# Two changes of order and one of shape in a two-layer streaming encoder: the sums for seven products, and the mixer's kernel product in column quarters

## The chip, the cores and the metric

The kernel runs on one core of one Trainium2 chip. The metric is the device time of one launch in microseconds (us), taken as the median of three runs; one further execution was profiled.

## What is computed

One inference step of a two-layer streaming encoder, for a prompt of 1024 positions and a sample of 64, 1088 columns in all, with 1024 channels. Layer 0 mixes tokens by sliding-window attention, layer 1 by a complex-diagonal state space (S5). Each layer ends in a gated feed-forward part with a causal depthwise convolution of width 3:

```python
def conv_ffn(h, prev, w_up, conv_w, conv_b, w_down):
    up = h @ w_up
    full = jnp.concatenate([prev.astype(up.dtype), up], axis=1)
    ...
    y = (jax.nn.gelu(c[..., :D_FF]) * c[..., D_FF:]) @ w_down
```

The mixer of layer 1 has 64 groups of 16 channels, with one state of 64 complex numbers per group:

```python
    xr = jnp.einsum('blgi,gpi->blgp', u_blk, bbr)
    xi = jnp.einsum('blgi,gpi->blgp', u_blk, bbi)
    ...
    y = jnp.einsum('blgp,gip->blgi', sr, cr) - jnp.einsum('blgp,gip->blgi', si, ci)
```

The kernel computes it over chunks of eight positions, and needs tables for that: the response of every group over eight steps (16 by 128 numbers a group, here called the kernel product, `kps`), and the transposed input weights (`wps`).

## The kernel before, in words

**Products.** The engines are called PE (TensorE, the matrix engine), DVE (VectorE), ACT (ScalarE), POOL (GpSimd) and SP (SyncE, which only issues transfers here). The 1088 columns are worked in three blocks of 384, 384 and 320. A float32 product is made of three fast ones (`mm3`, L223 to L225), with weights and data split into a high and a low part (L216, L194 for the weights). PSUM has six banks for these products and two small tiles, `sm0` and `sm1`.

**The feed-forward part** (`ffn`, L340). The up-projection goes over 22 tiles f: the products of rows f and 22 + f, their evacuation into `u`, the convolution (`conv`, L419 to L421), GELU, the product of both halves (L437) and its write to DRAM as `gd` (L438, L439). In layer 1 the tiles from f = 5 are made by seven products in place of eight (`seven`; L508 to L521 are the evacuations on DVE). The down-projection over the first 768 columns is also made by seven products (`pair`); for that it needs sums of quarters of its weights (`sums_w`, L355 to L362) and of `gd` (`sums_g`, L367 to L374).

**The sums.** Each is a generator with two steps. The first issues a load (L355, L367). The second is four DVE operations in place (L358 to L361, L370 to L373) and a write to DRAM (`sd`, `td`). `aside` is called twice in each tile, once between the two convolutions and once behind the gate, and calls `sums(j)` with j counting the calls. `starts` says at which j a generator's first step is taken: odd j for the weights, even j for `gd`; `jobs` says at which j the second is. Before, that is j + 1. Loads and writes are on SP's queue in layer 0 and on POOL's in layer 1. The tile `jt` of layer 0 has one place for the weights' sums and two for those of `gd`; in layer 1 `jw` and `jg` have one place each, so a load has to wait until the write before it has landed.

**The tables of layer 1's mixer** (`ssm_prep`, L1098) are made beside layer 0's up-projection, as its `side` work: eight blocks q of four pairs of groups, each with `ssm_chunk` (L1016) and `ssm_toeplitz` (L1086). In `ssm_chunk` DVE makes `ct` (L1034 to L1039) and, with `cmul`, `w` (L882 to L887); ACT writes the input weights of each pair of groups into a block-diagonal tile `bd` (L1048). PE then multiplies: eight products of `bd[:, g, c]` with `ct[:, g, c]`, which add up into one 128 x 128 result `kps` (L1062). Each stationary operand is 128 columns wide and holds numbers in 32 of them, the other columns being zero. DVE takes the result into `kt` (L1066, L1067), which goes to DRAM. Eight transposes of `w` (L1073) follow, c = 0 into `sm0`, the bank that `kps` had, and c = 1 into `sm1`; ACT copies them (L1074) and SP writes them to `prm` (L1075).

**What sets the order.** A planner fixes the order of the instructions on every engine and queue when the program is built. Each instruction gets the number of the moment at which it was written (`cur_priority`, which counts up); among those that its reckoning holds ready, an engine takes the lowest number. `later(LOW)` adds 1500 to the numbers of the side work. `order(x, first)` keeps x behind `first` on its engine without a wait on the chip. Tiles with the same tag share their places.

Of the kernel before, what the change touches and what calls it, by code (L numbers as in the profile page):

```python
# [8 lines left out]
F32 = mybir.dt.float32  # L9
F32R = mybir.dt.float32r  # L10
I32 = mybir.dt.int32
AF = mybir.ActivationFunctionType
# [3 lines left out]
P = 128  # L16
# [6 lines left out]
KF = DFF // P  # L23
# [20 lines left out]
class Core:  # L44
# [72 lines left out]
    @contextmanager  # L117
    def later(self, n):

        p = self.tc.cur_priority  # L120
        self.tc.cur_priority = p + n
        yield
        self.tc.cur_priority = p

    @contextmanager
    def boundary(self, nsq=2):
# [84 lines left out]
    behind = ()  # L211
# [128 lines left out]
    def ffn(self, i, h, rb, after, side=None, beside=lambda: None, x=None, g=None):  # L340

        nc, tc, a = self.nc, self.tc, self.a
# [37 lines left out]
        jobs = {}  # L380

        def sums(j):

            for x in jobs.pop(j, []):
                next(x, None)
            if j in starts:
                x = starts[j]
                next(x)
                jobs[j + 1] = [x]

        def u_tile(m):
            u = self.t4([P, T + 4], "u")
# [50 lines left out]
        def aside():  # L443

            j = next(turns) + 1
            if side is not None and j <= SIDE:
                with self.later(LOW):
                    next(side, None)
            sums(j - 1)
# [84 lines left out]
        for f in range(1, KF):  # L534
# [14 lines left out]
                us = up([f, KF + f, f + 1])  # L549
            gate(f, us)  # L550
            aside()
        for j in range(2 * KF, 2 * KF + 2):
            sums(j)
        if i == 1:
            ts_ctx.__exit__(None, None, None)
# [61 lines left out]
        def part(c):  # L617

            t0, n = BLK[2]
            k0 = KCUT[c]  # L620
            out = {}
            for sz, tag in GT[c]:
                if tag == "big":
                    x = self.big([P, 2, sz, n], "gt")
                else:
                    x = self.blk.tile([P, 2, sz, n], F32R, name="gt", tag=tag, bufs=4 if tag == "blkA" else 2)
                for j in range(0, sz, 2):
                    raw = self.t4([P, 2, n], "gr")
                    nc.sync.dma_start(raw, gd[:, k0 + j:k0 + j + 2, t0:])
                    split_units(x, slice(j, j + 2), raw)  # L630
                    for z in range(2):
                        out[k0 + j + z] = x, j + z
                k0 += sz
            return out
# [24 lines left out]
        with self.boundary():  # L659
# [3 lines left out]
            gs = part(0)  # L663
# [228 lines left out]
    def ssm_small(self):  # L892

        nc, a = self.nc, self.a
# [5 lines left out]
        sm = self.prep.tile([P, 1024], F32, name="sm0", tag="sm").rearrange("p (a q) -> p a q", a=32)  # L900
# [79 lines left out]
        c, s = cs, sn  # L980
        for k in range(10):
# [8 lines left out]
            c, s = (ph[:, 0, k - 2], ph[:, 1, k - 2]) if k > 1 else (ta[:, 8], ta[:, 9])  # L990
# [3 lines left out]
        for t, n, p0 in ((self.tq[:, :, 0:32], 16, 0), (self.tp[:, :, 18:36], 9, 4)):  # L994
            t = t.rearrange("p q (c k) -> p q c k", c=2)
            V.memset(t[:, :, 0, 0:1], 1.0)
            V.memset(t[:, :, 1, 0:1], 0.0)
            w, k = 1, p0
            while w < n:
# [3 lines left out]
                m = [m[:, i, :NPR * u].rearrange("p (q j) -> p q j", j=u) for i in range(2)]  # L1003
                self.cmul(V, [t[:, :, i, w:w + u] for i in range(2)], [t[:, :, i, 0:u] for i in range(2)], y, m)
                w, k = w + u, k + 1
        self.bd_ = self.prep.tile([P, 4, 2, P], F32, name="bd", tag="sm")
        V.memset(self.bd_, 0.0)
        self.dv = self.prep.tile([P, 24], F32, name="dv")
        nc.sync.dma_start(self.dv[:, 16:], a["s_d"])
# [6 lines left out]
    def ssm_chunk(self, q):  # L1016

        nc, a = self.nc, self.a
        G, V = nc.gpsimd, nc.vector
        gs = slice(4 * q, 4 * q + 4)  # L1020
        if q == 0:
            z = self.pt([P, 8, 112], "z0")
            G.memset(z, 0.0)
            nc.sync.dma_start(self.kd[:, 0:7].rearrange("(b p) t i -> p b (t i)", p=P), z)
        two = lambda t, o, n: (t[:, gs, o:o + n], t[:, gs, o + n:o + 2 * n])
        (ac, as_), (bbr, bbi), (cr, ci) = (two(self.tq, o, 16) for o in (0, 32, 64))
        (pr, pi), (bc, bs) = two(self.tp, 0, 9), two(self.tp, 18, 9)

        ct = self.pt([P, 4, 2, 9, 16], "ct")
        m = self.pm2()  # L1030
        m1, m2 = (m[:, i].rearrange("p (g t i) -> p g t i", t=9, i=16) for i in range(2))
        wide = lambda x: x[:, :, None, :].to_broadcast([P, 4, 9, 16])
        tall = lambda x: x[:, :, :, None].to_broadcast([P, 4, 9, 16])
        V.tensor_mul(m1, wide(cr), tall(pr))  # L1034
        V.tensor_mul(m2, wide(ci), tall(pi))
        V.tensor_sub(ct[:, :, 0], m1, m2)
        V.tensor_mul(m1, wide(cr), tall(pi))
        V.tensor_mul(m2, wide(ci), tall(pr))
        V.scalar_tensor_tensor(ct[:, :, 1], m1, -1.0, m2, op0=ALU.mult, op1=ALU.subtract)  # L1039
        oc = self.pt([P, 4, 2, 16, 8], "oc")  # L1040
        for c in range(2):
            nc.scalar.activation(oc[:, :, c], ct[:, :, c, 1:9].rearrange("p g t i -> p g i t"), AF.Copy)
        nc.sync.dma_start(self.prm[:, gs, OC:OC + 256], oc.rearrange("p g c i t -> p g (c i t)"))

        for e, r in enumerate((slice(0, 64), slice(64, 128))):
            o = self.bd_[r, 0, 0, 16 * e:16 * e + 1]
            o = bass.AP(tensor=o.tensor, offset=o.offset, ap=[o.ap[0], [2 * P + 32, 4], [P, 2], [1, 16]])
            nc.scalar.activation(o, self.tq[r, gs, 32:64].rearrange("p g (c j) -> p g c j", c=2), AF.Copy)  # L1048

        w = self.pt([P, 4, 2, 16, 8], "w")  # L1050
        m = self.pm2()
        m = [m[:, i, :512].rearrange("p (g j s) -> p g j s", j=16, s=8) for i in range(2)]
        row = lambda x: x[:, :, :, None].to_broadcast([P, 4, 16, 8])
        pwr = lambda x: x[:, :, None, 0:8].to_broadcast([P, 4, 16, 8])
        self.cmul(V, (w[:, :, 0], w[:, :, 1]), (row(bbr), row(bbi)), (pwr(pr), pwr(pi)), m)
        yield

        kps = self.sm_ps("kps", 0)
        behind = self.last_mm
        for g in range(4):  # L1060
            for c in range(2):
                x = nc.tensor.matmul(kps[:, :P], self.bd_[:, g, c], ct[:, g, c, 0:8].rearrange("p t i -> p (t i)"),  # L1062
                                     start=g + c == 0, stop=g + c == 4)
                self.order(x, behind)
        kt = self.prep.tile([P, P], F32, name="kt")
        V.scalar_tensor_tensor(kt[:, 0:16], self.dv[:, :16], self.dv[:, 16 + q:17 + q], kps[:, 0:16], op0=ALU.mult, op1=ALU.add)  # L1066
        V.tensor_copy(kt[:, 16:], kps[:, 16:P])  # L1067
        nc.sync.dma_start(self.kd[q * P:q * P + P, 7:].rearrange("j t i -> j (t i)"), kt)
        b3 = self.pt([P, 4, 2, P], "b3")
        for c in range(2):  # L1070
            wps = self.sm_ps("wps", c)
            for g in range(4):
                self.order(nc.tensor.transpose(wps[:, g * P:g * P + P], w[:, g, c].rearrange("p j s -> p (j s)"), self.ident), behind)  # L1073
            nc.scalar.activation(b3[:, :, c], wps.rearrange("p (g n) -> p g n", g=4), AF.Copy)  # L1074
        nc.sync.dma_start(self.prm[:, gs, OW:OW + 256], b3.rearrange("p g c n -> p g (c n)"))  # L1075

        tab = self.pt([P, 4, 2, 144], "tab")
        m = self.pm2()
        m = [m[:, i].rearrange("p (g b a) -> p g b a", b=9, a=16) for i in range(2)]
        v = lambda i: tab[:, :, i].rearrange("p g (b a) -> p g b a", a=16)  # L1080
        self.cmul(G, (v(0), v(1)), (wide(ac), wide(as_)), (tall(bc), tall(bs)), m)
        G.tensor_copy(tab[:, :, :, 129:138], tab[:, :, :, 0:9])
        for c, o in enumerate((OCO, OSI)):
            nc.gpsimd.dma_start(self.prm[:, gs, o:o + 138], tab[:, :, c, 0:138])
# [515 lines left out]
```

## Time and profile before

| | |
|---|---|
| median of three runs | 2259.97 us (2258.63 to 2260.15) |
| the profiled execution's own time | 2264.88 us |
| its span | 2263.1 us |
| PE, DVE, ACT, POOL busy | 2201.7, 1688.5, 1019.2, 415.2 us |
| instructions | 36074 |

The span runs from the first to the last instruction on the core; the time of the execution holds 1.8 us more around it. Busy time counts each engine by itself. A product's duration runs until its results are out, so products that follow each other overlap, and their cost is the distance of their starts. The columns of a timeline are the start, the duration, the engine and line, the operation, its output and inputs, the part of the array that it uses (rows*columns), the moving operand and the count of instructions put together; [idle before <- what ended it] stands behind those that found the engine idle. One float32 product that isn't split shows as two instructions.

### The profile page before, as it was taken

What the parts mean: (1) busy time and instruction counts of PE and PEld (TensorE: products, weight loads), DVE (VectorE), ACT (ScalarE), POOL (GpSimd) and SP (SyncE); (2) the same over time, 40 slices, a digit from 0 to 9 for tenths busy, and PEclk for the clock granted to TensorE, in tenths of its full rate; (3) what the DMA queues carried; (4) which work ended last, traced back from release to release, by engine and by line L of the source; (5) the groups of instructions that cost most, each with busy time, mean ns of one, the idle gap of its engine ahead of it and who ended that gap; (6) DMA issues with size and microseconds to landing.
All of it is one profiled execution on the core that took longest, in us unless ns stands there. A gap on an engine that the chain in (4) does not pass through costs nothing. (4 is left out here: it accounts for less than half of the span.)

```text
span 2263.1 us, 36074 instructions
## 1 busy us (share of the span) xinstructions
PE 2201.7 (97%) x13875; PEld 2122.4 (94%) x13875; DVE 1688.5 (75%) x2954; ACT 1019.2 (45%) x1839; POOL 415.2 (18%) x474
## 2 busy tenths in 40 slices
PE   8999999999999999999998899999999999999997
PEld 8987789999999999999996799999999999989997
DVE  8677647989877777667767855588997787686764
ACT  5255747422333343455534641263544444355543
POOL 5322004200042423000200034352011011100000
PEclk9999999999999999999998999999999999999999
DMA  5100014656345565887749888652266577578773
GB/s 195 37 21 29 16 65 151 242 191 211 107 138 185 178 203 179 259 288 222 227 164 339 262 286 300 234 166 74 96 233 218 213 287 258 193 250 278 222 256 99
DMA packets 208124, 428.48 MB, mean 189 GB/s; under 512 B 23312, under 2 KB 114224, under 8 KB 205008
## 3 DMA queue, kind: packets, MB, share of 16 engines
q1 hardware_dynamic: 175648, 326.56, 44.0%
q0 software_dynamic: 23984, 95.12, 11.6%
q10 hardware_dynamic: 8320, 4.49, 0.9%
q8 instruction: 109, 1.79, 0.3%
q14 instruction: 63, 0.52, 0.1%
HBM read 297.75 MB, written 128.37 MB: 188 GB/s over the span
## 5 line engine op out<-in xcount | busy, mean ns | idle before, releaser
L223 PE MATMUL mm<-hl,whl 128*128 128x384 f32 (+1 forms) x1960 | 643.8, 329 | 7.7 <-DVE hl L306 3.1
L225 PE MATMUL mm<-hh,whl 128*128 128x384 f32 (+1 forms) x1960 | 641.1, 328 | 2.3 <-DVE whl L216 2.3
L224 PE MATMUL mm<-hh,whl 128*128 128x384 f32 (+1 forms) x1960 | 642.2, 328 | 0.0
L223 PEld LDWEIGHTS mm<-hl,whl 128*128 128x128 f32 x1960 | 368.4, 188 | 10.8 <-DVE hl L306 4.5
L225 PEld LDWEIGHTS mm<-hh,whl 128*128 128x128 f32 x1960 | 368.4, 188 | 2.9 <-DVE whl L216 2.9
L224 PEld LDWEIGHTS mm<-hh,whl 128*128 128x128 f32 x1960 | 368.7, 188 | 0.0
L216 ACT ACTIVATE whl<-raw 128x1024 fp32r<-128x1024 f32 x202 | 212.9, 1058 | 339.1 <-PE mm L225 176.4
L216 DVE TENSOR_TENSOR whl<-raw,whl 128x1024 fp32r<-128x1024 f32 x202 | 254.4, 1263 | 96.7 <-ACT whl L216 96.2
L223 PE MATMUL mm<-gt,whl 128*128 128x384 f32 (+1 forms) x968 | 318.5, 329 | 7.9 <-DVE y L613 3.6
L225 PE MATMUL mm<-gt,whl 128*128 128x384 f32 (+1 forms) x968 | 316.9, 328 | 0.7 <-DVE whl L216 0.7
L224 PE MATMUL mm<-gt,whl 128*128 128x384 f32 (+1 forms) x968 | 317.3, 328 | 0.0
L223 PEld LDWEIGHTS mm<-gt,whl 128*128 128x128 f32 x968 | 182.9, 189 | 10.5 <-DVE y L613 4.9
L225 PEld LDWEIGHTS mm<-gt,whl 128*128 128x128 f32 x968 | 182.7, 189 | 1.0 <-DVE whl L216 1.0
L224 PEld LDWEIGHTS mm<-gt,whl 128*128 128x128 f32 x968 | 182.8, 189 | 0.0
L194 DVE TENSOR_TENSOR whl<-raw,whl 128x1024 fp32r<-128x1024 f32 x84 | 96.3, 1153 | 73.0 <-ACT whl L193 72.4
L193 ACT ACTIVATE whl<-raw 128x1024 fp32r<-128x1024 f32 x84 | 82.6, 986 | 126.8 <-DMA raw<-sd 51.0
L419 ACT ACTIVATE t<-u,ppt 128x1090 f32<-128x1090 f32 x88 | 114.2, 1298 | 50.6 <-DVE u L521 24.6
L420 DVE SCALAR_TENSOR_TENSOR t<-u,ppt,t 128x1090 f32<-128x1090 f32 x88 | 123.6, 1406 | 9.8 <-ACT t L419 9.1
L421 DVE SCALAR_TENSOR_TENSOR t<-u,ppt,t 128x1090 f32<-128x1090 f32 x88 | 123.4, 1403 | 0.4
L563 DVE TENSOR_TENSOR gt<-gr,gt 128x768 fp32r<-128x768 f32 (+2 forms) x106 | 90.2, 880 | 10.7 <-ACT gt L562 10.1
L331 POOL TENSOR_TENSOR y<-y,xl 128x768 f32<-128x768 f32 (+1 forms) x16 | 31.3, 1954 | 354.0 <-DVE y L328 288.0
L562 ACT ACTIVATE gt<-gr 128x768 fp32r<-128x768 f32 (+2 forms) x106 | 78.3, 771 | 39.5 <-DMA gr<-gd 30.2
(390 smaller groups left out, 4181.0 us busy)
## 6 DMA issues: line engine op xcount, KB each, us to landing
raw<-in_w_up SPq DMA_DIRECT2D x88, 512.0 KB, 4.3
raw<-in_w_down SPq DMA_DIRECT2D x74, 512.0 KB, 4.5
raw<-sd SPq DMA_DIRECT2D x40, 512.0 KB, 4.6
sj<-in_w_up POOLq DMA_DIRECT2D x68, 256.0 KB, 6.4
su<-sj POOLq DMA_DIRECT2D x34, 512.0 KB, 5.8
raw<-su SPq DMA_DIRECT2D x34, 512.0 KB, 4.8
pm<-prm SPq DMA_DIRECT2D x32, 522.0 KB, 8.2
gr<-td SPq DMA_DIRECT2D x40, 384.0 KB, 5.9
```

The lines of the kernel that those rows point to most:

```text
L193: nc.scalar.activation(w[:, 0], raw, AF.Copy)
L194: nc.vector.tensor_sub(w[:, 1], raw, w[:, 0].bitcast(F32))
L216: x = nc.scalar.activation(w[:, 0], raw, AF.Copy), nc.vector.tensor_sub(w[:, 1], raw, w[:, 0].bitcast(F32))
L223: nc.tensor.matmul(out, w[:, 0, sl], xl, start=start, stop=False)
L224: nc.tensor.matmul(out, w[:, 0, sl], xh, start=False, stop=False)
L225: self.last_mm = nc.tensor.matmul(out, w[:, 1, sl], xh, start=False, stop=stop)
L331: x = by[q].tensor_add(yq, yq, xs[q])
L419: nc.scalar.activation(t, u[:, 0:T + 2], AF.Identity, bias=cb(m), scale=cw(0, m))
L420: nc.vector.scalar_tensor_tensor(t, u[:, 1:T + 3], cw(1, m), t, op0=ALU.mult, op1=ALU.add)
L421: self.last_conv = nc.vector.scalar_tensor_tensor(t, u[:, 2:T + 4], cw(2, m), t, op0=ALU.mult, op1=ALU.add)
L562: nc.scalar.activation(x[:, 0, u], raw, AF.Copy)
L563: nc.vector.tensor_sub(x[:, 1, u], raw, x[:, 0, u].bitcast(F32))
```

## The change

- `due(p)` is new: instructions written under it get the number p, and the count goes on behind it as if they had not been there.
- The second step of a sum is taken at j + 2 in place of j + 1; the last round of calls is one longer.
- `bd` shrinks from 128 to 32 columns for each g and c, and L1048 writes it with a plain slice.
- The kernel product of g goes into partitions 32 g to 32 g + 31 of `kps`, from a stationary operand of 32 columns. c is now the outer loop, each quarter adds up two products, and all eight have one number.
- The transposes of c = 1 come first, with the number of the kernel product plus 12; those of c = 0 have that number plus 50.

```diff
@@ -123,6 +123,14 @@
     @contextmanager
+    def due(self, p):
+
+        q = self.tc.cur_priority
+        self.tc.cur_priority = p
+        yield
+        self.tc.cur_priority = q
@@ -386,7 +394,7 @@
                 x = starts[j]
                 next(x)
-                jobs[j + 1] = [x]
+                jobs[j + 2] = [x]
@@ -549,7 +557,7 @@
             aside()
-        for j in range(2 * KF, 2 * KF + 2):
+        for j in range(2 * KF, 2 * KF + 3):
             sums(j)
@@ -1003,7 +1011,7 @@
-        self.bd_ = self.prep.tile([P, 4, 2, P], F32, name="bd", tag="sm")
+        self.bd_ = self.prep.tile([P, 4, 2, 32], F32, name="bd", tag="sm")
@@ -1043,9 +1051,7 @@
         for e, r in enumerate((slice(0, 64), slice(64, 128))):
-            o = self.bd_[r, 0, 0, 16 * e:16 * e + 1]
-            o = bass.AP(tensor=o.tensor, offset=o.offset, ap=[o.ap[0], [2 * P + 32, 4], [P, 2], [1, 16]])
-            nc.scalar.activation(o, self.tq[r, gs, 32:64].rearrange("p g (c j) -> p g c j", c=2), AF.Copy)
+            nc.scalar.activation(self.bd_[r, :, :, 16 * e:16 * e + 16], self.tq[r, gs, 32:64].rearrange("p g (c j) -> p g c j", c=2), AF.Copy)
@@ -1057,20 +1063,25 @@
-        for g in range(4):
-            for c in range(2):
-                x = nc.tensor.matmul(kps[:, :P], self.bd_[:, g, c], ct[:, g, c, 0:8].rearrange("p t i -> p (t i)"),
-                                     start=g + c == 0, stop=g + c == 4)
+
+        due = self.tc.cur_priority
+        for c in range(2):
+            for g in range(4):
+                with self.due(due):
+                    x = nc.tensor.matmul(kps[32 * g:32 * g + 32, :P], self.bd_[:, g, c], ct[:, g, c, 0:8].rearrange("p t i -> p (t i)"),
+                                         start=c == 0, stop=c == 1)
                 self.order(x, behind)
...
         b3 = self.pt([P, 4, 2, P], "b3")
-        for c in range(2):
+        for c in (1, 0):
             wps = self.sm_ps("wps", c)
             for g in range(4):
-                self.order(nc.tensor.transpose(wps[:, g * P:g * P + P], w[:, g, c].rearrange("p j s -> p (j s)"), self.ident), behind)
+                with self.due(due + (50 if c == 0 else 12)):
+                    x = nc.tensor.transpose(wps[:, g * P:g * P + P], w[:, g, c].rearrange("p j s -> p (j s)"), self.ident)
+                self.order(x, behind)
             nc.scalar.activation(b3[:, :, c], wps.rearrange("p (g n) -> p g n", g=4), AF.Copy)
```

## Rows read from the trace of the kernel before

**Rows 1.** The page, part 1: busy time, share of the span, instructions.

```profile
PE 2201.7 (97%) x13875; PEld 2122.4 (94%) x13875; DVE 1688.5 (75%) x2954; ACT 1019.2 (45%) x1839; POOL 415.2 (18%) x474
```

**Rows 2.** Waits of PE, 590 to 905 us: total us, times, longest.

```profile
PE wps L1073 <- DVE kt L1067: 4.4, 3, 1.7
PE wps L1073 <- DVE w L887: 2.9, 3, 1.2
```

**Rows 3.** Waits of DVE, 1790 to 2040 us.

```profile
DVE jg L370 <- DMA jg<-gd: 31.3, 7, 7.2
```

**Rows 4.** Waits of PE, 1310 to 2010 us.

```profile
PE mm L223 <- DVE u L520: 4.9, 3, 2.1
```

**Rows 5.** Timeline of PE, 656 to 664 us: start, us, what, [idle before].

```profile
656.09 0.39 PE L1062 MATMUL kps<-ct,bd 128*128 128x128 f32 x2
...
656.46 0.38 PE L1062 MATMUL kps<-ct,bd 128*128 128x128 f32 x2
...
657.57 0.31 PE L223 MATMUL mm<-hl,whl 128*128 128x320 f32 x1
...
658.59 0.31 PE L224 MATMUL mm<-hh,whl 128*128 128x320 f32 x1
...
662.66 0.63 PE L1073 MATMUL wps<-ident,w 128*128 128x128 f32 x4 [1.68 <-DVE kt L1067]
```

**Rows 6.** Timeline of PE, 1280 to 1309 us: half-column runs (128*64).

```profile
1283.22 1.16 PE L1249 MATMUL p<-U,pm 128*64 128x137 f32 x16
1284.31 0.73 PE L1309 MATMUL p<-U,pm 128*128 128x137 f32 x4
1284.88 0.56 PE L230 MATMUL p<-ppt,ident 128*128 128x238 f32 x2
...
1288.73 0.69 PE L1249 MATMUL p<-U,pm 128*64 128x137 f32 x8
1289.35 0.74 PE L1309 MATMUL p<-U,pm 128*128 128x137 f32 x4
```

**Rows 7.** Timeline of PE, 120.3 to 121.4 us.

```profile
120.53 0.31 PE L225 MATMUL gq<-hh,whl 128*128 128x320 f32 x1
120.78 0.65 PE L796 MATMUL po<-ptT,vt 128*64 128x256 f32 x4
```

**Rows 8.** Timeline of PE, 776 to 783 us.

```profile
776.35 0.31 PE L225 MATMUL mm<-hh,whl 128*128 128x320 f32 x1
777.88 0.33 PE L1073 MATMUL wps<-ident,w 128*128 128x128 f32 x1 [1.22 <-DVE w L887]
...
781.65 0.63 PE L1073 MATMUL wps<-ident,w 128*128 128x128 f32 x4 [1.44 <-DVE kt L1067]
```

**Rows 9.** Timeline of PE, 772.2 to 772.9 us.

```profile
772.36 0.38 PE L1062 MATMUL kps<-ct,bd 128*128 128x128 f32 x2
```

**Rows 10.** Timeline of DVE, 764 to 784 us.

```profile
771.86 0.69 DVE L884 TENSOR_TENSOR w<-m 128x512 f32<-128x512 f32 x1 [2.81 <-DMA prm<-oc]
...
777.13 0.69 DVE L887 TENSOR_TENSOR w<-m 128x512 f32<-128x512 f32 x1
...
781.25 0.26 DVE L1067 COPY kt<-kps 128x112 f32<-128x112 f32 x1
```

**Rows 11.** Tile jt: ns min/median/max, first and last start in us.

```profile
L358 DVE TENSOR_TENSOR jt<-jt x11: 679/691/694, 404.8 to 566.5; 128x512 f32<-128x512 f32 x11
```

**Rows 12.** Line L437 on DVE, 400 to 700 us.

```profile
L437 DVE TENSOR_TENSOR t<-t x12: 1284/1291/2149, 437.0 to 684.6; 128x1090 f32<-128x1090 f32 x12
```

**Rows 13.** Timeline of DVE, 1964 to 1990 us.

```profile
1980.13 0.56 DVE L370 TENSOR_TENSOR jg<-jg 128x384 f32<-128x384 f32 x1 [7.24 <-DMA jg<-gd]
```

**Rows 14.** Stretches: from:to, length, busy us (x instructions) of PE, PEld, DVE, ACT, POOL, then granted clock, DMA share, GB/s.

```profile
2070.00:2079.90 9.90, 8.13 (x47) 7.81 (x46) 6.14 (x7) 4.54 (x5) 0.00 (x0) 1.00 0.55 167
2079.90:2083.30 3.40, 3.40 (x12) 3.40 (x11) 3.23 (x5) 2.17 (x3) 0.00 (x0) 0.50 0.96 326
```

**Rows 15.** Timeline of PE, 1981 to 1984 us.

```profile
1983.40 0.44 PE L223 MATMUL mm<-hl,whl 128*128 128x384 f32 x1 [1.72 <-DVE u L520]
```

More of the change, by code (lines that the diff above doesn't have):

```diff
@@ L123, in later @@
         self.tc.cur_priority = p
+    @contextmanager
+    def due(self, p):
[3 more added lines that the diff above has]
+        self.tc.cur_priority = q
     @contextmanager
```

## The prediction, made before the change was run

> **What bounds the kernel now.** I read the busy shares first: the matrix engine (PE) is busy for 2201.7 of 2263.1 us [rows 1], so what counts is PE time and the idle time of PE; work on another engine counts only where PE waits for it. Then the waits of PE in the stretch in which the mixer's tables are prepared beside layer 0's up-projection, 590 to 905 us: PE waits there 7.3 us in all, six times, each time ahead of a transpose of `w` (L1073): 4.4 us for `kt` (L1067) and 2.9 us for `w` (L887) [rows 2]. All else there is PE at work, so each microsecond of PE time taken out of this stretch should come off the total. Last I read the sums: VectorE (DVE) stands 31.3 us ahead of L370 in layer 1, waiting for the load that it sums [rows 3]; PE waits 4.9 us in layer 1's up-projection for evacuations (L520) queued behind such a wait [rows 4].
>
> **Part 1: the kernel product by quarters.** Before, the eight products of a block alternate with those of the up-projection. From one kps row to the next with one 320-column product between them is 0.37 us (656.09 to 656.46); seven 320-column products alone take 657.57 to 658.59, 0.146 us each [rows 5]. So one kps product costs 0.37 - 0.146 = 0.224 us, a block of eight 1.79 us, the eight blocks 14.3 us.
>
> After, each product fills 32 of the 128 columns, and four of them can stand in the matrix engine side by side. No row shows quarters; the nearest are halves. Sixteen half-column instructions (137 moving columns) take 1283.22 to 1284.31, 1.09 us, and eight take 1288.73 to 1289.35, 0.62 us [rows 6]. The difference, 0.47 us for eight, is 0.118 us for a pair, and 0.15 us is left for starting and draining. Four full-column instructions of the same length take 0.57 us (1284.31 to 1284.88, the first of them after a half-column run [rows 6]), of which 4 x 0.118 = 0.47 us is streaming: two halves stream in the time of one full instruction, and coming back to full width costs 0.10 us. Going in costs as much: the last 320-column product ahead of a half-column run takes 0.25 us (120.53 to 120.78 [rows 7]) in place of 0.146.
>
> If four quarters go in parallel as two halves do, sixteen instructions are four steps of 128 columns (0.110 us each by length): 0.44 + 0.15 + 0.10 + 0.10 = 0.79 us a block. It saves 1.79 - 0.79 = 1.00 us, **8.0 us in eight blocks**. The bounds: if only two go in parallel, eight steps, 1.23 us, 4.5 us saved in all; if none, sixteen steps, 2.11 us, 2.6 us lost. I take four: halves lose nothing against full width in the rows. That eight come in one run, so that going in and out is paid once a block, I take from the order before: the alternation, one for one, is what consecutive numbers on both sides give [rows 5], and the change gives all eight one number.
>
> The Trainium skill speaks against the full factor: "TensorE: Matmul & The Clock Gate" (Part 3, measured speedup) has three column tiles at 2.38 times, not 3. Estimated from that share (0.79 of the factor), the four steps would take 0.56 in place of 0.44 us, and part 1 would save about 7.1 us. "TensorEngine Tiling (Array Packing)" (Key Properties) says that a change of tiling mode drains the engine; the 0.10 us in rows 6 and 7 agree.
>
> The smaller memset of `bd` and the plainer write of L1048 are on DVE and ScalarE ahead of the stretch, with PE at work beside them: nothing. They would cost only if kps came to wait for `bd`, and no row of PE's waits names it [rows 2].
>
> **Part 2: the order of the transposes.** The c = 0 transposes reuse the bank that `kt` reads. Before, they go as soon as the planner thinks `kt` done, and PE then stood 1.68 and 1.44 us for L1067 [rows 5, 8]; all three such waits make 4.4 us [rows 2]. After, they are 50 products behind the block: 0.79 + 50 x 0.146 + 0.45 us for the four c = 1 transposes = 8.5 us after its start. In the worst row the block starts at 772.36 [rows 9] and L1067 ends at 781.51 [rows 10], 9.2 us; but there the c = 1 transposes wait too and carry c = 0 past that. **4.4 us go.** What waits behind c = 0 is the copy L1074 and the write of `prm`; PE needs neither in this stretch. The synchronising engine's queue may stand at that write, but two weight units are loaded ahead.
>
> The c = 1 transposes come earlier, and that costs. Before, 7 + 9 products and the block lie ahead of them: 772.36 to 776.5, 4.1 us [rows 8, 9]. After, 12 products and the shorter block: 0.79 + 12 x 0.146 = 2.5 us, 1.6 us sooner. But `w` isn't sooner: L887 ended at 777.82 because L884 had waited 2.81 us for a DMA [rows 10]. Where PE already waits for `w`, in three blocks, the wait grows by up to 1.6 us, 4.8 us in all; in the other five it grows by 0 to 1.6 us, at most 8.0 us. Nothing at all is the lower end, if the planner knows that `w` is late and lets products go first. I take **3.5 us lost**, between nothing and the 4.8 us of the three, nearer to the latter, since before the order never gave way to `w`.
>
> **Part 3: the sums.** The change asks for the four DVE operations half a tile later. I forecast **0 us**. The queues don't follow the order of the program here: they take what is ready. L358 of layer 0 ran eleven times between 404.8 and 566.5 us, while the gates (L437) of tiles 0 to 11 ran from 437.0 to 684.6 [rows 11, 12]; the gates are 22.5 us apart, and the last of these sums, which stands in the program behind the gate of tile 10 (662 us), ran some 95 us ahead of it. So the sums run as soon as the planner thinks their load landed, and fill gaps of DVE; a later number loses a tie, no more. Loads, sums and writes of one buffer keep their own order on SyncE's and GpSimd's queues, and each load still follows the write that frees its buffer. After the last gate nothing lies between the steps 43 and 46, so the tail is the old one. The bounds: 4.9 us gained, if the L520 waits [rows 4] go; for the loss, see the third rival.
>
> **The sum.** -8.0 - 4.4 + 3.5 + 0 = -8.9 us. The profiled execution took 2264.88 us, its span 2263.1 us; the median of the runs is 2259.97 us, 4.9 us below, and the saving is taken off the median: **2251 us**. A measurement of this kernel can tell about 0.2%, 4.5 us, from no change; so faster is below 2255.5, slower above 2264.5.
>
> **Rivals.** *More is gained* (2243 us): the sums do leave their waits, 4.9 us, and `w` costs nothing, 3.5 us: 17.3 us in all. For it: L370 waits 7.24 us in the row at 1980.13 [rows 13], and half a tile is longer than that. Against it: the order by readiness of part 3.
>
> *The gain is eaten by `w`* (2257 us): the waits grow by 8 us, and one of them drops the clock. Of 12.4 us gained 4.4 stay, less 1.7. For it: behind a stretch in which PE had stood 1.8 of 9.9 us the granted clock was 0.50 (1.2 of 2.4 GHz) for 3.4 us [rows 14], 1.7 us lost. Against it: L884's wait for a DMA may shrink as the block moves.
>
> *Slower* (2268 us): in layer 1 the sums, now last in every tie, slip out of the gap of DVE ahead of L520 into the dense stretch of evacuations behind it. The wait of 7.24 us at 1980.13 cost PE only 1.72 us [rows 13, 15], because PE had free banks; among evacuations the whole 7.2 us would fall on PE, 5.5 us more each time. It decides from three of the eleven sums on: 16.5 - 8.9 = 7.6 us slower. Against it: a sum that isn't ready in the planner's reckoning isn't issued, and the gap comes in every tile.
>
> *The change doesn't do what it says* is, for the sums, my forecast itself; for the quarters it is the bound without overlap: 8.0 + 2.6 = 10.6 us less gain, 2262 us.
>
> **How the numbers follow.** The forecast (with two or four quarters in parallel, 2247 to 2255) has 0.55; more gained 0.15; eaten by `w`, or no overlap, 0.20; slower 0.10. So faster 0.70, same 0.20, slower 0.10. The range, 2243 to 2261 us, takes in the first three but for half of the second's spread and the slowest of the third.
>
> **What would show it.** Right: sixteen kps instructions with no other product between them, in 0.6 us or so; no PE wait for L1067; waits for L887 in three to five blocks; L370 still waiting for its load in layer 1, in the same place ahead of L520. Part 1 is wrong if such a run takes over 1.2 us, part 2 if c = 0 still waits, part 3 if the L370 waits are gone. The whole is wrong if PE's idle time in a stretch that the change doesn't touch (the S5 stage, the tails) moves by several microseconds.

## The result, and the profile after

The change is slower, by half a per cent: 2272.21 us (2268.38 to 2276.65, 5 runs) against 2260.15 us for the kernel before (2258.63 to 2265.68, 5 runs on the same chip), a ratio of 1.0049 [1.003, 1.0068], 11 us. Timed again on another chip (e16) it was 1.0069 [1.0049, 1.0089]. The profiled execution took 2274.5 us, span 2272.7 us. All ratios below are against the kernel before on the same chip; 0.0010 is 2.25 us. That kernel's own runs spread over 12 to 20 us on a chip (2244.93 to 2264.55 in 29 runs on one), so one profile alone doesn't settle a few microseconds. Two executions far out, one of e10 (4328 us) and one of the kernel before (2669 us), are in no ratio.

The page of the kernel after, part 1, answers to [rows 1]; below it, with total, times and longest in us, the waits of PE from 590 to 905 us, which answer to [rows 2]:

```profile
PE 2203.6 (97%) x13875; PEld 2118.0 (93%) x13875; DVE 1685.7 (74%) x2954; ACT 1019.8 (45%) x1839; POOL 413.8 (18%) x474
```

```profile
PE wps L1083 <- DVE w L895: 10.5, 6, 3.5
PE wps L1083 <- DVE kt L1076: 1.0, 2, 0.6
```

PE is not less busy than before. The waits for `kt` are nearly gone, 4.4 to 1.0 us; those for `w` grew from 2.9 to 10.5 us, in six blocks in place of three. The timeline of PE in the block of [rows 8, 9] (start, duration, what, idle before):

```profile
773.01 0.31 PE L232 MATMUL mm<-hh,whl 128*128 128x320 f32 x1
773.25 0.41 PE L1071 MATMUL kps<-ct,bd 128*32 128x128 f32 x2
773.58 0.41 PE L233 MATMUL mm<-hh,whl 128*128 128x320 f32 x1
773.93 0.64 PE L1071 MATMUL kps<-ct,bd 128*32 128x128 f32 x14
774.50 0.42 PE L231 MATMUL mm<-hl,whl 128*128 128x320 f32 x1
774.75 0.30 PE L232 MATMUL mm<-hh,whl 128*128 128x320 f32 x1
...
779.84 0.48 PE L1083 MATMUL wps<-ident,w 128*128 128x128 f32 x1 [3.47 <-DVE w L895]
```

Two things are to be seen. The eight quarter products don't stand in one run: one goes alone, a product of the up-projection follows, then the other seven. It is so in seven of the eight blocks. From 773.01 to 774.75 are 1.74 us with three 320-column products of 0.147 us in them, so the block costs 1.30 us. And the c = 1 transposes wait 3.47 us. DVE there, same columns:

```profile
773.82 0.69 DVE L892 TENSOR_TENSOR w<-m 128x512 f32<-128x512 f32 x1 [1.39 <-DMA prm<-oc]
...
779.10 0.69 DVE L895 TENSOR_TENSOR w<-m 128x512 f32<-128x512 f32 x1
```

In [rows 10] the last step of `w` started 4.8 us behind the first kps product (777.13 against 772.36); here it is 5.9 us, while PE asks for it sooner. The stretches around this wait (length, busy us of PE, PEld, DVE, ACT and POOL, then the granted clock) show what came on top:

```profile
771.50:778.30 6.80, 4.87 (x40) 3.87 (x38) 5.41 (x8) 1.21 (x2) 0.00 (x0) 1.00 0.77 270
778.30:785.10 6.80, 5.26 (x19) 5.24 (x20) 6.47 (x12) 4.46 (x7) 2.86 (x2) 0.50 0.21 82
785.10:791.90 6.80, 6.80 (x41) 6.75 (x41) 4.60 (x5) 0.78 (x3) 4.08 (x3) 1.00 0.56 198
```

Behind the wait the clock was half (1.2 of 2.4 GHz) for 6.8 us; the 5.26 us that PE worked in them are worth 2.6.

The sums moved nothing. Waits of DVE from 1790 to 2050 us, then of PE from 1310 to 2030 us, which answer to [rows 3, 4]:

```profile
DVE jg L378 <- DMA jg<-gd: 28.5, 6, 6.8
```

```profile
PE mm L231 <- DVE u L528: 4.5, 3, 2.2
```

The rest of the loss lies behind the stretch. Where the up-projection of layer 0 ends, the chain of the last block of tables is late. The kernel before, from the timelines of SP's queue and of ACT (these rows were not read for the prediction):

```profile
900.90 0.58 SPq L1075 DMA_DIRECT2D prm<-b  x1
907.46 5.09 SPq L1094 DMA_DIRECT2D tl<-kd  x8
912.64 0.53 SPq L374 DMA_DIRECT2D td<-jt  x1
```

```profile
914.53 2.01 ACT L1095 ACTIVATE tp<-tl 128x1024 f32<-128x1024 f32 x1 [14.74 <-DMA tl<-kd]
...
928.29 3.05 ACT L562 ACTIVATE gt<-gr 128x768 fp32r<-128x768 f32 x4
```

The kernel after:

```profile
907.50 0.37 SPq L1086 DMA_DIRECT2D prm<-b  x1
914.22 0.33 SPq L382 DMA_DIRECT2D td<-jt  x1
914.71 7.39 SPq L1105 DMA_DIRECT2D tl<-kd  x8
922.20 1.12 SPq L582 DMA_DIRECT2D gr<-gd  x2
```

```profile
924.07 2.01 ACT L1106 ACTIVATE tp<-tl 128x1024 f32<-128x1024 f32 x1 [16.60 <-DMA tl<-kd]
...
934.93 3.05 ACT L570 ACTIVATE gt<-gr 128x768 fp32r<-128x768 f32 x4
```

The c = 0 transposes of the last block come 36 products behind those of c = 1, so the write of `prm` is issued 6.6 us later. The loads of `tl` stand behind it on SP's queue, and now also behind `td`, the write of a sum, which the planner has put ahead of them (before, it came behind). That write waited for DVE's last step of the sum until 914.2 us, while `prm` had landed at 911.7: of the delay of the loads, 7.3 us, some 3 are the queue's order. ACT stands in `tp` for the loads, and behind `tp` on ACT stand the splits of weights and of `gt`, the data of layer 0's first seven products, 6.6 us later too (2.2 us of it is what the stretch itself had lost by then).

PE meets this lateness well behind its start. Its waits from 905 to 1050 us in the kernel after:

```profile
PE mm L231 <- DVE y L621: 2.6, 1, 2.6
PE mm L231 <- DVE gt L571: 0.3, 1, 0.3
```

For `gt` itself PE waits only 0.3 us. The wait for `y`, an evacuation of the seven products, ends at 1038 us. The evacuation stands on DVE behind a low half of weights whose load is late: ACT splits these weights from 1034.57 us, where it did from 1027.79 before, and the evacuation starts at 1037.67 where it started at 1030.89 (PE waited 0.8 us for `y` then). Behind this wait the clock was half for 6.8 us once more.

### The profile page after: what moved, and what is told of

Its sections match the earlier page's. It is cut to its first block, busy times and chain, and to the rows that moved or that the text cites. A ratio compares the mean times of both kernels' runs of the same rounds, so it can differ in the third digit from the quotient of the medians.

```text
span 2272.7 us, 36081 instructions
## 1 busy us (share of the span) xinstructions
PE 2203.6 (97%) x13875; PEld 2118.0 (93%) x13875; DVE 1685.7 (74%) x2954; ACT 1019.8 (45%) x1839; POOL 413.8 (18%) x474
## 5 line engine op out<-in xcount | busy, mean ns | idle before, releaser
L224 ACT ACTIVATE whl<-raw 128x1024 fp32r<-128x1024 f32 x202 | 213.0, 1058 | 348.3 <-PE mm L233 173.2
L419 DVE TENSOR_TENSOR u<-rb,mm 128x384 f32<-128x384 f32 (+1 forms) x164 | 80.6, 505 | 22.6 <-PE mm L233 17.7
```

The source lines that it names most:

```text
L224: x = nc.scalar.activation(w[:, 0], raw, AF.Copy), nc.vector.tensor_sub(w[:, 1], raw, w[:, 0].bitcast(F32))
L419: nc.vector.tensor_mul(u[:, t0 + 2:t0 + 2 + np_], rb[:, t0:t0 + np_], ps[:, :np_])
```

## The experiments

Eighteen runs were made, one of them (e16) of the change again, on five chips: e1 to e4, e5 to e8, e9 to e12, e13 to e16, and e17 with e18. The table gives each ratio, and from each one's single profile: the waits of PE for `w` and `kt` in the side stretch, and the time from the 4250th to the 5250th instruction of `mm3` (the start of layer 0's down-projection, about 900 to 1075 us) and the longest wait of PE in S5's chunks (about 1205 to 1310 us).

| kernel | ratio, 95% interval | w, kt us | 4250 to 5250 | longest in S5 |
|---|---|---|---|---|
| before | 1 | 2.9, 4.4 | 174.5 | 2.1 |
| after | 1.0049 [1.0030, 1.0068] | 10.5, 1.0 | 180.4 | 4.1 |
| e1 sums alone | 1.0009 [0.9995, 1.0024] | 1.8, 3.6 | 173.2 | 2.6 |
| e2 change without the sums | 1.0043 [1.0027, 1.0058] | 5.6, 0.7 | 176.9 | 3.4 |
| e3 quarters alone | 1.0011 [0.9994, 1.0028] | 2.6, 3.2 | 174.0 | 3.3 |
| e4 transposes alone | 1.0042 [1.0024, 1.0061] | 6.0, 0.3 | 178.8 | 2.1 |
| e5 e4, c = 1 late | 1.0051 [1.0036, 1.0066] | 0, 2.6 | 181.0 | 2.1 |
| e6 e4, c = 0 early | 1.0012 [0.9997, 1.0027] | 2.5, 2.8 | 173.2 | 1.9 |
| e7 e4, last block old | 1.0019 [1.0007, 1.0031] | 4.1, 0.3 | 173.2 | 2.1 |
| e8 quarters in one run | 1.0027 [1.0015, 1.0040] | 2.7, 6.5 | 173.2 | 3.8 |
| e9 e8, S5 kept | 0.9976 [0.9960, 0.9993] | 3.0, 3.9 | 173.5 | 2.1 |
| e10 e5, last block old | 1.0015 [1.0003, 1.0027] | 0.7, 3.5 | 173.2 | 2.1 |
| e11 before, S5 moved | 1.0033 [1.0016, 1.0049] | 0.6, 2.3 | 173.2 | 3.7 |
| e12 e9 and e10 | 1.0008 [0.9997, 1.0019] | 5.5, 3.7 | 173.2 | 2.1 |
| e13 change, S5 kept | 1.0058 [1.0041, 1.0075] | 7.6, 1.3 | 181.6 | 2.0 |
| e14 change, last block old | 1.0055 [1.0035, 1.0074] | 8.0, 2.3 | 173.6 | 4.2 |
| e15 change, both | 1.0024 [1.0014, 1.0035] | 6.1, 2.7 | 174.7 | 2.2 |
| e16 the change again | 1.0069 [1.0049, 1.0089] | 10.2, 1.4 | 177.1 | 3.7 |
| e17 e15, old transposes | 1.0014 [0.9998, 1.0030] | 0.9, 4.5 | 173.7 | 2.6 |
| e18 e17, one run | 1.0002 [0.9986, 1.0017] | 2.0, 7.2 | 175.1 | 2.3 |

**The parts by themselves.** e1 takes the sums alone, e2 the rest of the change, e3 the quarters, e4 the transposes.

e1:

```diff
-                jobs[j + 1] = [x]
+                jobs[j + 2] = [x]
-        for j in range(2 * KF, 2 * KF + 2):
+        for j in range(2 * KF, 2 * KF + 3):
```

> Only the sums' second step moves to j + 2; tables as before. Theory A (the whole loss is in the transposes of w, which now come ahead of w and stop PE): within 4 us of before, 2256 to 2264; in layer 1 L370 still stands for its load in the same place (about 31 us in all), and PE's waits for L520 stay near 4.9 us. Theory B (the sums, last in every tie, hand their buffers back late and cost PE in the tails of both layers): 2265 to 2272, with PE waits of over 2 us at the start of layer 0's seven products, near 1036 us.

e2 is the change with these lines as before.

> Quarters, one number for the eight products, transposes at 12 and 50; the sums as before. Theory A: as slow as the changed kernel, 2267 to 2274; PE waits 8 to 12 us for w (L887 before, L895 after) between 590 and 905 us, and one wait over 3 us takes the clock to half for some us. Theory B: near or below before, 2250 to 2260.

The shape of `bd` and of the products is the change's; e3 keeps the old loop of the transposes and sets `self.tc.cur_priority = due + 8` behind the block, so that later numbers are the old ones.

> Quarters with one number, but the transposes keep their old numbers (8 counted on behind the products); sums as before. Theory A: part 1 alone gains 4 us (0.5 us a block, since in seven of eight blocks one product stands alone ahead of the other seven, and going in and out is paid twice), but the shorter block brings the transposes 0.5 us nearer to w, so PE's waits for w grow from 2.9 to 4 to 7 us; 2255 to 2261. Theory B: 2250 to 2257.

e4:

```diff
-        for c in range(2):
+        for c in (1, 0):
...
+                with self.due(due + (50 if c == 0 else 12)):
```

> The eight products at full width and alternating as before; only the transposes get their new order and numbers (12 and 50). Theory A: here is the loss: PE's waits for w grow from 2.9 to 6 to 9 us, those for kt go from 4.4 to under 1.5; 2259 to 2268. Theory B: 4 us gained, 2254 to 2258, with no more waiting for w than before.

The transposes carry a loss by themselves (9.5 us), the sums nothing that can be told from none, and the quarters gain nothing, though their profile has 8.6 us less of PE busy than that of before (2193.1 against 2201.7). e2 is slow, as theory A had it, but without the waits that it named: 5.6 us for `w` in place of 8 to 12, and none over 1.6 us.

**The transposes: w or the late write.** e5 moves c = 1 back, e6 moves c = 0 forward, e7 leaves the last block alone.

```diff
 e5  due + (50 if c == 0 else 45)
 e6  due + (16 if c == 0 else 12)
 e7  due + ((11 if c == 0 else 16) if q == 7 else 50 if c == 0 else 12), c = 0 first where q == 7
```

> The transposes alone, as in e4, with both halves late: c = 1 gets the number +45 instead of +12 (19 to 25 products behind the block, 36 in the last), c = 0 keeps +50. PE should wait less for w (6.0 us in e4, 2.9 us before) and still not for kt; the write of prm stays as late as in e4. Theory W (the loss comes from c = 1 going before w is there): the loss goes, and with the kt waits of 4.4 us also gone the time is 2 to 6 us below the kernel before. Theory L (the loss comes from the late write of prm in the last block, which holds up the synchronising engine's queue and with it the first weights of layer 0's down-projection): still slower than before by 4 to 10 us, with a PE gap of 2 to 4 us between 920 and 945 us.

> The transposes alone with c = 1 early as in e4 (+12) and c = 0 soon behind it (+16 instead of +50: 13 products behind c = 1 in every block, where e4 has 18 to 24, and 36 in the last). Theory W: slower than before by 5 to 10 us, as e4 (9.5 us), since c = 1 still waits 5 to 7 us for w. Theory L: the write of prm in the last block is issued near its old time (900.9 us) and no gap of PE stands at the start of the down-projection, so the loss goes: within 3 us of the kernel before.

> e4 with the last of the eight blocks alone put back to the old order and numbers (c = 0 first); blocks 0 to 6 have the transposes as in e4. Theory L: the loss goes, 0 to 4 us below the kernel before (seven blocks keep what the kt waits gave), and PE idles less than 1 us between 910 and 945 us. Theory W: seven of the eight early c = 1 remain, so 4 to 9 us slower than before, w waits of 5 to 6 us.

e5 has no wait for `w` left and is as slow as e4; e6 and e7 lose most of the loss. (In e6 the waits for `w` shrank as well, 6.0 to 2.5 us, so e6 alone doesn't tell the theories apart.) So theory L holds: the late write is the greater part, 0.0023 to 0.0036 of the time (e4 less e7, e5 less e10; each pair is on two chips, with some 0.002 to either side), 5 to 8 us. For e5, SP's queue, then the waits of PE from 905 to 950 us, then ACT:

```profile
906.35 0.32 SPq L382 DMA_DIRECT2D td<-jt  x1
906.76 0.39 SPq L1086 DMA_DIRECT2D prm<-b  x1
```

```profile
PE mm L231 <- DVE gt L571: 4.6, 1, 4.6
```

```profile
925.21 2.00 ACT L1106 ACTIVATE tp<-tl 128x1024 f32<-128x1024 f32 x1 [11.12 <-DMA tl<-kd]
931.38 3.04 ACT L570 ACTIVATE gt<-gr 128x768 fp32r<-128x768 f32 x4
```

e6's ACT:

```profile
913.00 2.01 ACT L1106 ACTIVATE tp<-tl 128x1024 f32<-128x1024 f32 x1 [14.11 <-DMA tl<-kd]
926.59 3.05 ACT L570 ACTIVATE gt<-gr 128x768 fp32r<-128x768 f32 x4
```

PE waits for the low part of `gt`, which DVE makes from ACT's half. What held the write in e5 is the queue more than the transposes: ACT had copied the last of them by 899.9 us (899.8 in the kernel before), but `td` stood ahead of the write and waited for DVE's sum until 906.3. In all six kernels with the late write (the change, e2, e4, e5, e13 and e16) `td` stands ahead of the loads of `tl`, in e4, e5 and e13 ahead of the write of `prm` too; in the other fourteen it stands behind both. e2, e4 and e5 have the sums as before, so it isn't their delay in the program that moves `td`. No run separates the late transposes from this order. PE's wait is for `gt` in e4, e5 and e13 (3.4 to 4.6 us) and mostly for `y` in the change, e2 and e16 (1.8 to 2.6 us). In the table the column from 4250 to 5250 separates the two kinds with no overlap: 176.9 to 181.6 us in the six kernels with the late write, 173.2 to 175.1 in the others. e7 is still above the kernel before, although only seven early c = 1 remain; what that rest is, these three don't say.

**The quarters: one run, and S5.** e8 is e3 with a lower number for the second to eighth product, to put them in one run.

```diff
-                with self.due(due):
+                with self.due(due - (c + g > 0)):
```

> The quarters alone, as in e3, but with the second to eighth product one number lower than the first, so that all eight stand in one run in every block instead of one, a product of the up-projection, and seven. If going in and out of the quarters is what e3 paid twice (1.30 against 0.79 us a block), the block takes 0.75 to 0.85 us and PE's time in 590 to 905 us falls by some 4 us against e3 and 8 us against the kernel before; the total is 4 to 8 us below the kernel before if PE's time there is what counts, and within 2 us of it if a transfer or the clock sets the end of the stretch.

The run is there, in every block. Timeline of PE of e8:

```profile
692.11 0.31 PE L232 MATMUL mm<-hh,whl 128*128 128x320 f32 x1
692.35 0.64 PE L1071 MATMUL kps<-ct,bd 128*32 128x128 f32 x16
692.92 0.41 PE L233 MATMUL mm<-hh,whl 128*128 128x320 f32 x1
693.17 0.31 PE L231 MATMUL mm<-hl,whl 128*128 128x320 f32 x1
```

From 692.11 to 693.17 less two products is 0.77 us a block. Yet e8 is 6 us slower than before. Its waits of PE from 1195 to 1310 us, in S5, which the edit doesn't touch:

```profile
PE p L1259 <- DVE wk L1307: 5.4, 2, 3.5
PE p L1259 <- DMA pm<-prm: 4.2, 3, 3.4
PE p L1319 <- ACT ys L1333: 3.8, 1, 3.8
```

The planner had put S5 in another order. On SP's queue of e8 two loads of U stand behind the write of `yf`:

```profile
1240.95 0.32 SPq L1345 DMA_DIRECT2D yf<-yd  x1
1241.44 2.19 SPq L1196 DMA_DIRECT2D U<-hd  x2
```

It had done so in every kernel with quarters, the change too. e9 adds a product that nothing reads, which happens to bring the old order back; e11 adds it to the kernel before, where it brings the new one.

```diff
+        for _ in range(1):
+            y = nc.tensor.matmul(kps[:, 256:256 + P], self.ident, self.ident, start=True, stop=True)
+            self.order(y, x)
```

> The quarters in one run, as in e8, with one more product of the identity by itself (128 columns, into columns 256 to 383 of kps, which nothing reads) behind each block. It costs 8 times some 0.2 us of PE, 1.8 us; with it the planner puts the S5 stage in the order of the kernel before, which every kernel with quarters so far had left (the loads of U, the write of yf and a copy of wk each some places from where they were). Theory S (the quarters gain 4 to 6 us in the side stretch and the other order of S5 gives them back): PE idles 17 to 19 us between 1150 and 1310 us instead of 21 to 24, and the time is 3 to 8 us below e8, 0 to 4 us below the kernel before. Theory Q (the quarters themselves gain nothing, or cost the clock): as e8, 4 to 8 us slower than before, plus the 1.8 us.

> The kernel before with its eight products on the whole width, and the same extra product of the identity behind each block, 1.8 us of PE. Here it has the opposite effect on the planner: S5 gets the order that it has in the kernels with quarters. Theory S: PE idles 21 to 24 us in S5 instead of 17.5 to 19, and the time is 4 to 9 us above the kernel before. Theory Q: 1 to 3 us above it, the price of the eight products.

e9's queue has the loads of U ahead of the write of `yf` again:

```profile
1232.78 1.71 SPq L1199 DMA_DIRECT2D U<-hd  x2
1242.69 0.33 SPq L1348 DMA_DIRECT2D yf<-yd  x1
```

The same product made one kernel 5.4 us faster than before and the other 7.4 us slower, as theory S has it: of the 7.4 some 5.6 would be S5's order, with 0.22 us for each added product, as for one of kps in the prediction. (e8 and e9 ran on different chips, each against its own runs of before.) In all twenty profiles the longest wait in S5 is 3.3 us or more with the new order and at most 2.6 with the old. Compared instruction by instruction, S5 has just two orders in them, but for a place or two on ACT: seven kernels have the new one, thirteen the old. The stage itself, from the 5250th to the 6000th instruction of `mm3`, takes 247.6 to 254.8 us with the new order, 250.0 on average, and 244.2 to 249.3 with the old, 246.7 on average. That is 3.3 us, not 5.6, and the ranges overlap (e11's own profile has 247.6, that of before 249.3), so by these two measures the order costs some 3 to 6 us; no single pair of profiles shows it. The 11 us between e8 and e9 are more than that; the side stretch has another order too, and PE waits 2.6 us less for `kt`. e9 is the one version that beats both kernels. That it gains by the quarters is less sure: e18 below is e9 with the sums and shows no gain.

**The faults taken out together.** e10 is e5 with the last block as in e7, e12 is e10 with e9's quarters and product.

> The transposes alone, in blocks 0 to 6 as in e5 (both halves 19 to 30 products behind the block), in the last block in the old order and at the old numbers, so that the write of prm isn't late. No wait for kt or w of more than 1 us in all in blocks 0 to 6 (7.3 us before), first 250 products of the down-projection in 41 us as before. If the two faults found so far (c = 1 ahead of w, the late write in the last block) are all that is wrong with the transposes: 3 to 7 us below the kernel before. If not: within 2 us of it or slower.

> What the change set out to do with the faults found taken out: the quarters in one run, the transposes as in e10, and the extra product behind each block that here too keeps S5 in its old order. By the parts: 6 us of PE saved by the quarters, 1.8 us paid for the extra products, up to 7 us of waits gone: 6 to 11 us below the kernel before by theory S. By theory Q no gain from the quarters: 0 to 5 us below e10 at most in the other direction, that is e10 plus 2 us.

Both missed. e10 has 4.2 us of waits left where 7.3 stood, and no gain; in e12, whose block is 1 us shorter but for the added product, `w` is late again, by 3.4 us in the last block:

```profile
PE wps L1087 <- DVE w L895: 5.5, 4, 3.4
PE wps L1087 <- DVE kt L1080: 3.7, 5, 1.0
```

So PE's time saved in a block is in part time by which `w` and `kt`, in DVE's order, are late. Then the change itself, as a table of two by two: e13 has the extra product, e14 the last block's old transposes, e15 both, e16 neither.

> The whole change with one extra product of the identity behind each block (1.8 us in eight), which keeps S5 in the order of the kernel before; the late transposes of the last block stay. If the two faults (other order of S5, late write of prm in the last block) add up: 2 to 6 us below the change itself, 5 to 9 us above the kernel before. S5 (products 5250 to 6000 of the up- and down-projections) 245 to 249 us instead of 250; a wait of PE at the start of the down-projection or in its 250 first products as in the change. If S5's order doesn't matter here: the change plus 1.8 us.

> The whole change with the last block's transposes back in the old order and at the old numbers; S5 is in the other order, as in the change. If the two faults add up: 5 to 9 us below the change, 2 to 6 us above the kernel before, products 4250 to 5250 in 173 to 175 us as in the kernel before, where the change takes 180. If the late write doesn't matter: as the change.

> The whole change with both faults out: the extra product behind each block and the last block's transposes as of old. If these two are what made the change slower: within 4 us of the kernel before, to either side, 8 to 13 us below the change. If a third cause of more than 4 us is in it: still 5 us or more above the kernel before.

> The change itself, unaltered, on the same chip as the three kernels before this one in the list: 8 to 13 us above the kernel before, as measured at first (1.0049).

Of e16's 0.0069 the S5 order takes away 0.0011, the last block 0.0014, the two together 0.0045 (10 us; with the extra products' price taken off, more). They matter, and not as a plain sum; the intervals, some 0.002 to either side, don't tell whether that is chance (e14 was expected 5 to 9 us below the change and is 3 below). 0.0024 is left, and e15's PE still shows the wait that stood first in the change:

```profile
777.96 0.33 PE L1086 MATMUL wps<-ident,w 128*128 128x128 f32 x1 [2.97 <-DVE w L895]
```

e17 is e15 with the loop of the transposes as before, and e18 has the one run too.

> e15 (the whole change with S5 in its old order and the last block's transposes as of old) with the transposes of blocks 0 to 6 in the old order and at the old numbers too; the quarters (split in two runs, as in the change), the sums and the extra product stay. If the early c = 1 transposes of seven blocks are the third cause: waits for w fall from 6.1 us to some 3 us, kt waits rise to some 4 us, no wait of PE over 2 us in the side stretch, and the time is 4 to 8 us below e15: 2 us above to 3 us below the kernel before. If the third cause lies in the quarters or the sums: as e15, 4 to 7 us above the kernel before.

> e17 with the eight quarter products of every block in one run (the second to eighth one number lower): e9 with the sums. If a split block pays for going in and out twice: 2 to 5 us below e17, 3 to 7 us below the kernel before, as e9 (5.3 us below). If the split costs nothing: as e17.

e17 falls to 1.0014 and e18 to 1.0002; the waits for `w` fall as expected, but each step is within the intervals, and e18, expected 3 to 7 us below the kernel before, isn't below it. By their direction the early c = 1 is the third cause, some 2 us; that isn't settled.

## Why the prediction was wrong, point by point

**Part 1, -8.0 us.** The rate was right: quarters in one run cost 0.77 us a block against the 0.79 worked out, so four go in parallel. The figure of the Trainium skill weighed against it, three column tiles at 2.38 times in "TensorE: Matmul & The Clock Gate" (Part 3, measured speedup), would by the prediction's estimate ask for 0.12 us more a block; the trace doesn't show that loss. What failed is the step "That eight come in one run ... I take from the order before": one number for all eight did not do it, the block came in two runs, and going in and out is paid twice, 1.30 against 0.77 us. In the Trainium skill, "TensorEngine Tiling (Array Packing)" (Key Properties) says that changing the tiling mode drains the engine; the trace agrees in that each change has a price, 0.10 us. So 7 x 0.49 and, in the one block that was whole, 1.0, 4.4 us of PE were saved in place of 8.0.

**Part 2, kt, -4.4 us.** Right: 3.4 of 4.4 went. **w, +3.5 us.** Mis-sized: 7.6 us, and 2.6 us by the half clock behind the longest wait. The term took the waits to grow by the 1.6 us that PE comes sooner, in three blocks; they grew in six, since `w` moved back as well. With these sizes the stretch comes to -4.4 - 3.4 + 7.6 + 2.6 = +2.4 us; from the 2500th to the 4250th instruction of `mm3` the profiles have 321.5 us after and 319.3 before, +2.2. The rival *eaten by w* had this mechanism and, with 8 us and a drop of the clock, nearly its size.

**What waits behind c = 0, costed at nothing.** This step failed. "PE needs neither in this stretch" holds for blocks 0 to 6 but not for the end of the stretch. The cover named, "two weight units are loaded ahead", was too short: on SP's queue the write, and a sum's write that the planner put ahead, held the loads of `tl`, and on ACT `tp` stands ahead of the splits for the next stage. It measured 5 to 8 us where the transposes changed alone; in the change itself, 3 us with S5's new order (e16 less e14) and 8 with the old (e13 less e15), each with 4 to 6 us to either side. The rows of ACT and SP of the kernel before, shown above, were there to be read, though not that the planner would move a sum's write.

**S5.** No term of the sum had it. The prediction said it would be wrong "if PE's idle time in a stretch that the change doesn't touch (the S5 stage, the tails) moves by several microseconds", and it did: PE's idle time in the stage (5250th to 6000th instruction of `mm3`) went from 19.5 to 23.5 us. But the text gave no cause by which it could, and no price; the order costs some 3 to 6 us. e11 shows that eight small products, one a block and 300 us or more ahead of S5, are enough.

**Part 3, 0 us.** Right: e1 is 1.0009 [0.9995, 1.0024], in the change the waits for the loads of the sums are 28.5 us (31.3 before [rows 3]) and PE's waits behind them 4.5 us (4.9 [rows 4]). The rival *slower* by slipping sums, the only one on that side, didn't happen; the loss had other places.

**All together.** The forecast missed by 20 us, 8.9 less against 11 more. By the sizes above, as an estimate, part 1 accounts for 3.6 of it, `kt` for 1.0, `w` and the clock for 6.7, the late chain for 3 to 8 and S5 for 3 to 6, 17 to 25 us in all.

## What to carry to other kernels

Where instructions are delayed, follow what they feed to the last of the repeated blocks, where no next block covers it, and through every in-order queue on the way: a transfer that is late by 6.6 us held a copy on ACT, and that copy held the next stage's data. Look for transfers of other chains that a planner has put in between. Where a planner orders the program from a reckoning of times, a shorter block here may reorder a stage far away: compare the order of every engine and queue first, and time a part with that order held fixed. A saving on the busy engine counts only as far as its next operand is ready; here PE's saved time turned into waits for DVE.

## What the runs showed of the hardware

Four column quarters stream in the time of one product: sixteen instructions of 128 columns, 0.57 us from the first start to the next product's (692.35 to 692.92). A product next to such a run costs 0.24 to 0.25 us on either side in place of 0.146, and the one between a run of two instructions and a run of fourteen 0.35 (773.58 to 773.93). The clock went to half for 6.8 us at PE's 3.47 us wait, for 3.4 us at the 2.97 us of e15, and not at all at one of 3.3 us in the same place of e16, so the length of that one wait didn't decide it.
